# Encoder layer: layer norm of the convolution branch moved to the mixing stage, attention's steps issued further apart, last projections keys instead of values

## The chip, the cores and the metric

One core of a Trainium2 chip. The metric is the device time of one execution in microseconds; the time before is the median of 3 runs. Engines: PE (matmuls, weight loads), DVE (vector), ACT (scalar), POOL (GpSimd), SP (issues most transfers).

## The reference

One layer on 2048 tokens of width 1024, everything in float32. Attention looks at a window of 8 by 16 neighbours on a grid of 32 by 64 tokens, with 8 heads of 64 channels. Beside it runs a convolution branch of 512 channels: `conformer_conv` gates a with sigmoid(g), convolves over 31 positions, takes a layer norm over the 512 channels, and silu. 16 experts follow.

```python
        h = rms_norm(x, norm1_g[l])
        proj = jnp.einsum('bsd,de->bse', h, w_in[l])
        q, k, v, a, g = jnp.split(proj, splits, axis=-1)
        ...
        attn = neighbourhood_attention(q, k, v, rpb[l])
        conv = conformer_conv(a, g, conv_w[l], conv_b[l], conv_ln_g[l], conv_ln_b[l])
        mixed = jnp.concatenate([rms_norm(attn, attn_out_g[l]), rms_norm(conv, conv_out_g[l])], axis=-1)
        x = x + jnp.einsum('bse,ed->bsd', mixed, w_out[l])
        h = rms_norm(x, norm2_g[l])
        x = x + expert_choice_ffn(h, w_router[l], w_gate[l], w_up[l], w_down[l])
    return rms_norm(x, final_g)
```

## The kernel before

Products are made of three matmuls of split operands (`mm3`, L116: a rounded high part and the rest that `split` at L122 leaves). The program is written out in four stages, and each engine takes its instructions in the order of the source.

**Projections.** `jobs` (L376) lists what is projected: queries (`q_part`), keys (`k_part`), values (`v_part`) and the gated input of the convolution (`gate_a`). Results of q, k and v go to DRAM, from SP's queue (q, k) or ACT's (v). Beside them DVE does the 31 taps of the convolution (`conv_block`); `pump` doles them out by estimated time. A finished block of 128 channels is transposed and stored in `dw_scr` (`to_tokens`, put off by `LAG`). The last job is the second half of the values, and its last four parts stand in the attention loop.

**Attention.** 128 tiles: 8 heads, 4 column blocks, 4 row groups. The loop is a pipeline over tiles. Step i issues `transposes` of tile i + LT, `scores` of tile j = i + LS, `normed` of tile j - 1, `rests` of tile i + LT, `values` of tile i. In `scores` PE makes the products, DVE adds the bias and takes the minimum (L530), ACT takes the exponential and its sum (L534). `normed` takes a reciprocal on DVE (L544) and scales the tile (L546), even tiles on DVE, odd ones on POOL. `transposes` is PE, then a copy on ACT (L568). `rests` subtracts that copy on DVE (L573). `values` is PE (L586), and every fourth tile adds the two halves of the output: a copy on ACT (L596) and an addition on DVE (L599), at once.

```python
    LS, LT = 6, 2
```

Per head SP loads queries, keys (two parts), two bias tables and two sets of values, at fixed places in the loop: `load_qk` of the next head at tile 3 of this one, `load_kl` at 5, `load_tb` at 8, `load_v` at 13; `load_tb(h, 1)` at 0 and `load_v(h, 1)` at 3 are this head's own. `load` (L108) makes a transfer wait for the last matmul issued before it. The queries and keys lie in tiles of which one transfer fills 64 partitions, the values' transfers fill 24 or 32, the tables' 128. Tiles of 8 KB per partition come from a pool of 22 (`slot`), small ones from a pool of 8 (`e2`).

**What is done beside attention** is set by the table `on(i, ...)`. In the first 52 tiles it is the layer norm of the convolution branch: load a quarter of `dw_scr` (`conv_load`), statistics (`conv_stats`, L475), normalise (`conv_norm`: L483 on DVE, the gain and offset at L486 and L487 on POOL), store to `y_scr`. From tile 98 on it is loading, scaling (`wo_lead`, L501, POOL) and splitting (`wo_rest`, L506, DVE) of the output projection's weights.

**Mixing** goes over 16 groups of 128 tokens: `stage_y` loads y, `stage_z` takes silu and the sum of squares, `stage_b` transposes, `stage_a` splits the attention output (two groups at a time), `stage_c` multiplies with the weights in two halves, `stage_h`, `stage_d`, `stage_r`, `stage_s` make the router's scores (L710 is a power on POOL), `stage_k`, `stage_l` rank them. **Experts** are the rest, some 2290 us of matmuls.

Of the kernel before, what the change touches and what calls it, by code (L numbers as in the profile page):

```python
# [28 lines left out]
NORM_POOL = 2  # L29
# [25 lines left out]
def kernel(  # L55
# [100 lines left out]
    y_scr = dram.tile([4, P, 4, 512], F32, name="y_scr")  # L156
# [102 lines left out]
    def conv_block(i, u):  # L259

        a = slot([P, T])
        tap_w = lambda k: pv_sb[:, PV_CW + i * 31 + k : PV_CW + i * 31 + k + 1]

        def first():
            nc.vector.tensor_scalar(
                a, u, tap_w(15), pv_sb[:, PV_CB + i : PV_CB + i + 1], op0=ALU.mult, op1=ALU.add
            )

        def tap(k):
            sh = k - 15  # L270
# [5 lines left out]
        def to_tokens(b):  # L276
            ps = bank([P, 4, P])
            for j in range(4):
                tr(ps[:, j, :], a[:, (b * 4 + j) * P : (b * 4 + j + 1) * P], ident)
# [95 lines left out]

    jobs = [("q", 1), ("a", 1), ("q", 2), ("q", 3), ("a", 2), ("k", 0), ("k", 1), ("a", 3), ("k", 2), ("k", 3), ("v", 0), ("v", 1)]  # L376
    ws, raws = {}, {}

    def fetch(n):
# [48 lines left out]
    for n, (kind, i) in enumerate(jobs):  # L428
# [3 lines left out]
        if kind == "a":  # L432
            u = slot([P, T])
        for c in range(4):
# [5 lines left out]
            elif kind == "v":  # L440
                if i == 1 and c == 3:

                    break
# [22 lines left out]
    ys, ymv, wo = {}, {}, {}  # L466

    def conv_load(c):
        ys[c] = slot([P, 4, 512])
        ymv[c] = col(8, tag="mv")  # L470
        load(ys[c], dw_scr[c])

    def conv_stats(c, t):
        bst = col(6, tag="bs")
        nc.vector.bn_stats(bst, ys[c][:, t])  # L475
        nc.vector.bn_aggr(ymv[c][:, 2 * t : 2 * t + 2], bst)

    def conv_rstd(c):
        ymv[c, "r"] = rsqrt_mean(ymv[c].rearrange("p (r k) -> p r k", k=2)[:, :, 1], 1.0, 4)

    def conv_norm(c, t):
        y = ys[c][:, t]
        nc.vector.tensor_scalar(  # L483
            y, y, ymv[c][:, 2 * t : 2 * t + 1], ymv[c, "r"][:, t : t + 1], op0=ALU.subtract, op1=ALU.mult
        )
        nc.gpsimd.tensor_tensor(out=y, in0=y, in1=ln_gb[:, 0], op=ALU.mult)  # L486
        nc.gpsimd.tensor_tensor(out=y, in0=y, in1=ln_gb[:, 1], op=ALU.add)  # L487

    def conv_store(c):
        nc.gpsimd.dma_start(y_scr[c], ys[c])  # L490
# [48 lines left out]
    def normed(i):  # L539
# [5 lines left out]
        eng = nc.gpsimd if i % NORM_POOL else nc.vector  # L545
# [29 lines left out]
    def values(i):  # L575
# [747 lines left out]
```

## Time and profile before

| | |
|---|---|
| median of 3 runs | 3306.64 us (3303.76 to 3307.41) |
| the profiled execution | 3305.04 us |
| its span | 3303.3 us |
| PE busy in the span | 3154.7 us (96%) |
| DVE, ACT, POOL busy | 64%, 41%, 13% |
| attention (465.4 to 777.5 us) | 312.1 us, PE busy 224.3 |
| mixing (777.5 to 1010) | 232.5 us, PE busy 226.7 |

The span runs from the first to the last instruction of the profiled execution; all times of the trace count from its start. Durations below are of this execution, so a sum is made against 3305.04. The averages hide the stages: PE is full in projections, mixing and experts, and not in attention.

### The profile page before, as it was taken

What the parts mean: (1) busy time and instruction counts of PE and PEld (TensorE: products, weight loads), DVE (VectorE), ACT (ScalarE), POOL (GpSimd) and SP (SyncE); (2) the same over time, 40 slices, a digit from 0 to 9 for tenths busy, and PEclk for the clock granted to TensorE, in tenths of its full rate; (3) what the DMA queues carried; (4) which work ended last, traced back from release to release, by engine and by line L of the source; (5) the groups of instructions that cost most, each with busy time, mean ns of one, the idle gap of its engine ahead of it and who ended that gap; (6) DMA issues with size and microseconds to landing.
All of it is one profiled execution on the core that took longest, in us unless ns stands there. A gap on an engine that the chain in (4) does not pass through costs nothing.

```text
span 3303.3 us, 51326 instructions
## 1 busy us (share of the span) xinstructions
PE 3154.7 (96%) x21282; PEld 2890.9 (88%) x21282; DVE 2103.1 (64%) x3235; ACT 1369.5 (41%) x2216; POOL 433.7 (13%) x300
## 2 busy tenths in 40 slices
PE   7999996778997999999999999999999999999998
PEld 6888885667886999999999999999999999999997
DVE  5799967886555687555555555555555555555565
ACT  5111124564332444444444444444444444444454
POOL 2111015544322000000000000000000000000011
PEclk9999997898997999999999999999999999999999
DMA  6222377893344565656656565656656656566585
GB/s 249 61 86 90 112 207 206 226 238 109 119 140 138 200 194 183 212 181 216 195 201 189 194 215 189 199 189 204 204 189 196 203 193 212 177 209 198 198 277 201
DMA packets 394761, 610.88 MB, mean 185 GB/s; under 512 B 14240, under 2 KB 315552, under 8 KB 390304
## 3 DMA queue, kind: packets, MB, share of 16 engines
q1 hardware_dynamic: 358816, 555.11, 51.6%
q0 software_dynamic: 10080, 38.80, 4.5%
q10 hardware_dynamic: 25632, 13.70, 1.4%
q8 instruction: 167, 2.74, 0.4%
q14 instruction: 66, 0.54, 0.1%
HBM read 532.05 MB, written 75.50 MB: 184 GB/s over the span
## 4 chain that ended last, share of the span: by engine, by line
PE 67%; DMA 1%; DVE 0%; ACT 0%; issue 0%; POOLq 0%; POOL 0%; ACTq 0%
PE b L103 66%; PE b L106 1%; DMA s<-acc 0%; DMA s<-h_scr,c 0%; DMA out_dram<-s,c 0%; ACT s L123 0%; DVE s L124 0%; DVE s L1215 0%; DVE e L864 0%; DVE s L1220 0%; POOLq L1319 0%; DVE rd L870 0%; POOL c L144 0%; DVE e L1032 0%; ACT e L123 0%
## 5 line engine op out<-in xcount | busy, mean ns | idle before, releaser
L103 PE MATMUL b<-s,s 128*128 128x256 f32 (+1 forms) x15616 | 2249.3, 302 | 5.4 <-ACT s L211 4.2
L103 PEld LDWEIGHTS b<-s,s 128*128 128x128 f32 x15616 | 2076.1, 192 | 116.3 <-ACT s L211 4.6
L124 DVE TENSOR_TENSOR s<-s,s 128x1024 fp32r<-128x1024 f32 x768 | 896.4, 1221 | 116.0 <-ACT s L123 104.2
L123 ACT ACTIVATE s<-s 128x1024 fp32r<-128x1024 f32 x768 | 755.0, 1046 | 33.8 <-issue 30.1
L103 PE MATMUL b<-s,e 128*128 128x512 f32 x3072 | 746.8, 392 | 0.0
L103 PEld LDWEIGHTS b<-s,e 128*128 128x128 f32 x3072 | 560.6, 189 | 105.7
L1031 ACT ACTIVATE e<-b 128x256 f32<-128x256 f32 x256 | 98.3, 384 | 988.5 <-PE b L103 988.5
L1032 DVE TENSOR_TENSOR e<-e,b 128x256 f32<-128x256 f32 x256 | 107.8, 421 | 578.9 <-ACT e L1031 578.9
L272 DVE SCALAR_TENSOR_TENSOR s<-s,pv_sb,s 128x2033 f32<-128x2033 f32 (+14 forms) x120 | 311.4, 2595 | 2.2
L1061 POOL DMA_INDIRECT acc<-s,c x30 | 53.9, 1796 | 1249.4 <-ACT s L1058 1141.1
L586 PE MATMUL b<-s,s 128*128 128x256 f32 (+3 forms) x512 | 117.1, 331 | 83.0 <-DVE s L573 66.5
L124 DVE TENSOR_TENSOR e<-e,e 128x256 fp32r<-128x256 f32 x256 | 108.8, 425 | 123.8 <-ACT e L123 123.3
L586 PEld LDWEIGHTS b<-s,s 128*128 128x128 f32 (+1 forms) x512 | 93.6, 223 | 107.3 <-DVE s L573 86.0
L123 ACT ACTIVATE e<-e 128x256 fp32r<-128x256 f32 x256 | 106.9, 417 | 130.7 <-DVE e L1032 130.7
L972 POOL DMA_INDIRECT s<-h_scr,c x32 | 56.1, 1753 | 766.3 <-issue 655.6
L534 ACT ACTIVATE e<-e,c 128x384 f32<-128x384 f32 (+2 forms) x128 | 79.4, 620 | 97.7 <-DVE c L544 69.6
L546 POOL TENSOR_SCALAR e<-e,c 128x384 f32<-128x384 f32 (+1 forms) x64 | 82.7, 1292 | 190.4 <-DVE c L544 182.5
L106 PE MATMUL b<-ident,e 128*128 128x128 f32 (+1 forms) x512 | 95.5, 312 | 4.8 <-POOL e L546 4.1
L124 DVE TENSOR_TENSOR s<-b,s 128x512 fp32r<-128x512 f32 x80 | 52.4, 687 | 70.3 <-ACT s L123 70.3
L530 DVE CUSTOM_DVE_ANT_0 e<-b,s 128x384 f32<-128x384 f32 (+2 forms) x128 | 71.1, 556 | 24.5 <-PE b L103 24.0
L123 ACT ACTIVATE e<-b 128x256 fp32r<-128x256 f32 (+1 forms) x48 | 21.8, 454 | 145.8 <-PE b L103 96.2
L573 DVE TENSOR_TENSOR s<-b,s 128x384 fp32r<-128x384 f32 (+3 forms) x128 | 77.6, 606 | 6.5 <-ACT s L568 6.5
(140 smaller groups left out, 1520.3 us busy)
## 6 DMA issues: line engine op xcount, KB each, us to landing
s<-in_w_gate_dram SPq DMA_DIRECT2D x128, 1024.0 KB
s<-in_w_up_dram SPq DMA_DIRECT2D x128, 1024.0 KB
s<-in_w_down_dram SPq DMA_DIRECT2D x128, 1024.0 KB
s<-in_x_dram SPq DMA_DIRECT2D x8, 1024.0 KB
s<-in_xT_dram SPq DMA_DIRECT2D x8, 1024.0 KB
v_scr<-e ACTq DMA_DIRECT2D x32, 256.0 KB
s<-kh_scr SPq DMA_DIRECT2D x16, 512.0 KB
s<-kl_scr SPq DMA_DIRECT2D x16, 512.0 KB
```

The lines of the kernel that those rows point to most:

```text
L103: pe[0] = nc.tensor.matmul(o, l, r, start=start, stop=stop)
L106: pe[0] = nc.tensor.transpose(o, i, idt)
L123: nc.scalar.activation(hi, src, AF.Copy)
L124: nc.vector.tensor_tensor(lo, src, hi.bitcast(F32), op=ALU.subtract)
L272: nc.vector.scalar_tensor_tensor(a[:, s:e], u[:, s + sh : e + sh], tap_w(k), a[:, s:e], op0=ALU.mult, op1=ALU.add)
L530: nc.vector.tensor_tensor_reduce(out=s[:, :n], in0=ps[:, :n], in1=bt[:, boff : boff + n], scale=-1.0, scalar=3.0e38, op0=ALU.add, op1=ALU. ...
L534: nc.scalar.activation(s[:, :n], s[:, :n], AF.Exp, bias=nm[:, rg : rg + 1], scale=-1.0, accum_out=rs_[:, rg : rg + 1])
L546: eng.tensor_scalar(s[:, :n], s[:, :n], ri, None, op0=ALU.mult)
L573: nc.vector.tensor_tensor(lo, src, hi.bitcast(F32), op=ALU.subtract)
L586: nc_mm = nc.tensor.matmul(o[:, r0 : r0 + nr], vt[:nk, g], part[:nk, at : at + nr], start=g == 0 and p == 0, stop=g == 7 and p == 1, skip_ ...
L1031: nc.scalar.activation(s, ps[:, 0], AF.Silu)
L1032: nc.vector.tensor_tensor(s, s, ps[:, 1], op=ALU.mult)
```

## The change

- The layer norm leaves attention's table. `dw_scr` itself is loaded in the mixing stage (`stage_y`, a quarter at a time), each group of 128 tokens is normalised there (`stage_n`, `stage_o`), three groups ahead of `stage_c`; the first three stand in attention's tiles 117 to 121. `y_scr` is gone.
- The order of jobs: values are done before the last two key blocks, which are one job ("kk") done side by side; their last quarter stands in the attention loop at steps -5 and -3. Head 0's loads are issued from the start of that job on.
- `LS, LT` become 7, 3, and the halves of the output are copied one tile later (`out_copy`) and added two tiles later (`out_add`).
- Tiles below 100 are all scaled on POOL; from 100 on even ones on DVE as before.
- `stage_a` splits one group at a time; the convolution's accumulator is taken from the pool when it is first used; the last block's `to_tokens` come after 5 instead of 9.

```diff
-NORM_POOL = 2
+NORM_POOL = 100
...
-                later.append((now[0] + LAG + 4 * b, lambda b=b: to_tokens(b)))
+                later.append((now[0] + (LAG if i < 3 else 5) + 4 * b, lambda b=b: to_tokens(b)))
...
-    jobs = [("q", 1), ("a", 1), ("q", 2), ("q", 3), ("a", 2), ("k", 0), ("k", 1), ("a", 3), ("k", 2), ("k", 3), ("v", 0), ("v", 1)]
+    jobs = [("q", 1), ("a", 1), ("q", 2), ("q", 3), ("a", 2), ("k", 0), ("a", 3), ("k", 1), ("v", 0), ("v", 1), ("kk", 2)]
...
+        if kind == "kk":
+            load_qk(0)
...
+            elif kind == "kk":
+                if c == 3:
+
+                    break
+                for s in range(2):
+                    k_part(i + s, w[s], c)
+                    pump(4.4)
+                if c == 0:
+                    load_kl(0)
+                    load_tb(0, 0)
+                    load_v(0, 0)
+                    load_tb(0, 1)
...
-        eng = nc.gpsimd if i % NORM_POOL else nc.vector
+        eng = nc.gpsimd if i < NORM_POOL or i % 2 else nc.vector
...
         if k == 3:
             del pts[h, cb]
...
+            on(i + 1, lambda: out_copy(h, cb))
+            on(i + 2, lambda: out_add(h, cb))
...
-    def stage_y(t):
-        ym[t] = e2([P, 512])
-        nc.sync.dma_start(ym[t], y_scr[t // 4, :, t % 4])
+    def stage_y(c):
+        ym[c] = slot([P, 4, 512])
+        nc.sync.dma_start(ym[c], dw_scr[c])
+
+    def stage_n(t):
+
+        st = col(8, tag="mv")
+        nc.vector.bn_stats(st[:, 0:6], ym[t // 4][:, t % 4])
+        nc.vector.bn_aggr(st[:, 6:8], st[:, 0:6])
+        yn[t] = (st[:, 6:7], rsqrt_mean(st[:, 7:8], 1.0))
+
+    def stage_o(t):
+
+        y = ym[t // 4][:, t % 4]
+        mu, r = yn.pop(t)
+        nc.vector.tensor_scalar(y, y, mu, r, op0=ALU.subtract, op1=ALU.mult)
+        nc.gpsimd.tensor_tensor(out=y, in0=y, in1=ln_gb[:, 0], op=ALU.mult)
+        nc.gpsimd.tensor_tensor(out=y, in0=y, in1=ln_gb[:, 1], op=ALU.add)
...
-    LS, LT = 6, 2
...
-    for c in range(4):
-        o = 12 * c
-        on(o, lambda c=c: conv_load(c))
-        for t in range(4):
-            on(o + 7 + t, lambda c=c, t=t: conv_stats(c, t))
-            on(o + 12 + t, lambda c=c, t=t: conv_norm(c, t))
-        on(o + 10, lambda c=c: conv_rstd(c))
-        on(o + 16, lambda c=c: conv_store(c))
+    LS, LT = 7, 3
...
+    for t in range(3):
+        on(117 + t, lambda t=t: stage_n(t))
+        on(119 + t, lambda t=t: stage_o(t))
...
-        if -4 <= i < 0:
-            v_part(1, *w, 16 + i)
+        if i in (-5, -3):
+            k_part(2 + (i == -3), w[i == -3], 3)
...
     for t in range(0, 16):
-        if t + 3 < 16:
-            stage_y(t + 3)
         if t + 1 < 16:
             stage_b(t + 1)
-        if t % 2 == 1 and t < 15:
-            stage_a((t + 1) // 2)
+        if t + 3 < 16:
+            stage_n(t + 3)
         if t >= 1:
             stage_h(t - 1)
-        if t + 2 < 16:
-            stage_z(t + 2)
+        if t + 1 < 16:
+            stage_a(t + 1)
         if t >= 2:
             stage_s(t - 2)
         stage_c(t, 0)
+        if t + 3 < 16:
+            stage_o(t + 3)
+        if t % 4 == 0 and t < 12:
+            stage_y(t // 4 + 1)
+        if t + 2 < 16:
+            stage_z(t + 2)
```

SP's queue where projections end, before (`raw` is a weight tile, `s` a tile of the pool of 22, the sources are DRAM):

```order
L222 DMA raw_2386<-in_w_in_dram 128x8x256
L110 DMA s_2992<-qh_scr 64x2048
L110 DMA s_2992<-ql_scr 64x2048
L110 DMA s_2995<-kh_scr 64x2048 x2
L110 DMA s_2998<-kl_scr 64x2048 x2
L110 DMA s_3125<-in_tb_dram 128x1920
L110 DMA s_3127<-in_tb_dram 128x1280
L110 DMA s_3129<-v_scr 24x1024 x8
L110 DMA s_3373<-v_scr 32x1024 x8
L110 DMA s_3382<-qh_scr 64x2048
```

and of the change:

```order
L221 DMA raw_2603<-in_w_in_dram 128x8x256
L110 DMA s_3092<-qh_scr 64x2048
L110 DMA s_3092<-ql_scr 64x2048
L110 DMA s_3095<-kh_scr 64x2048 x2
L320 DMA kh_scr<-e_3123 128x512
L321 DMA kl_scr<-e_3124 128x512
L320 DMA kh_scr<-e_3155 128x512
L321 DMA kl_scr<-e_3156 128x512
L110 DMA s_3161<-kl_scr 64x2048 x2
L110 DMA s_3164<-in_tb_dram 128x1920
L110 DMA s_3166<-v_scr 24x1024 x8
L110 DMA s_3175<-in_tb_dram 128x1280
```

Head 0's values are read after a whole job of keys instead of right after the last values are written; stores of keys for heads 4 to 7 now stand between the loads.

DVE in two tiles of attention with a head's output due, before (line 483 is the layer norm):

```order
L530 ISA e_4402,c_4370<-b_4399,s_4160 128x512
L530 ISA c_4370 128x1
L544 RECIPROCAL c_4405<-c_4371 128x1
L546 TENSOR_SCALAR e_4375<-e_4375,c_4405 128x384
L573 TENSOR_TENSOR s_4366<-b_4393,s_4365 96x2x2x128
L599 TENSOR_TENSOR s_3279<-b_4329,e_4411 64x32x16
L530 ISA e_4423,c_4370<-b_4420,s_4160 128x512
L530 ISA c_4370 128x1
L544 RECIPROCAL c_4426<-c_4371 128x1
L573 TENSOR_TENSOR s_4366<-b_4414,s_4365 96x2x2x128
L483 TENSOR_SCALAR s_4128<-s_4128,c_4129,c_4391 128x512
```

and of the change (517, 531, 560, 597 are the former 530, 544, 573, 599):

```order
L517 ISA e_4478,c_4473<-b_4475,s_4288 128x288
L517 ISA c_4473 128x1
L531 RECIPROCAL c_4481<-c_4377 128x1
L560 TENSOR_TENSOR s_4469<-b_4464,s_4468 128x3x128
L597 TENSOR_TENSOR s_3334<-b_4360,e_4462 64x32x16
L517 ISA e_4499,c_4473<-b_4496,s_4288 128x384
L517 ISA c_4473 128x1
L531 RECIPROCAL c_4502<-c_4474 128x1
L560 TENSOR_TENSOR s_4469<-b_4490,s_4468 128x2x2x128
```

The scaling and the layer norm are gone from DVE here, and the addition of the output's halves stands two tiles after the values it adds.

POOL in one step of mixing, before:

```order
L710 TENSOR_TENSOR c_6832<-euler,c_6832 128x16
L144 TENSOR_TENSOR rcnorm<-c_6851,nhalf 128x1
L144 TENSOR_TENSOR ranorm<-c_6882,nhalf 128x1
L144 TENSOR_TENSOR c_6956<-c_6954,nhalf 128x1
L710 TENSOR_TENSOR c_6969<-euler,c_6969 128x16
```

and of the change (725 is the former 710; 630 and 631 are the gain and offset):

```order
L725 TENSOR_TENSOR c_6910<-euler,c_6910 128x16
L144 TENSOR_TENSOR c_6927<-c_6925,nhalf 128x1
L144 TENSOR_TENSOR ranorm<-c_6968,nhalf 128x1
L630 TENSOR_TENSOR s_6574<-s_6574,gains 128x512
L631 TENSOR_TENSOR s_6574<-s_6574,gains 128x512
L144 TENSOR_TENSOR rcnorm<-c_6993,nhalf 128x1
L144 TENSOR_TENSOR c_7052<-c_7050,nhalf 128x1
L725 TENSOR_TENSOR c_7065<-euler,c_7065 128x16
```

Two passes over 512 elements and one more small power stand in POOL's queue in every step, ahead of the power for the convolution half's norm two groups on (`rcnorm`) and of the one for the router's norm (`c`).

## Rows read from the trace of the kernel before

**Rows 1.** The page's part 1: busy time, share of the span, instructions.
```profile
PE 3154.7 (96%) x21282; PEld 2890.9 (88%) x21282; DVE 2103.1 (64%) x3235; ACT 1369.5 (41%) x2216; POOL 433.7 (13%) x300
```

**Rows 2.** Windows: attention, then mixing. Columns: stretch, length, busy (count) by engine, PEclk, DMA share, GB/s.
```profile
465.40:777.50 312.10, 224.31 (x1315) 198.36 (x1312) 244.04 (x683) 177.53 (x431) 157.80 (x122) 0.84 0.79 220
777.50:1010.00 232.50, 226.68 (x1305) 193.11 (x1305) 126.90 (x303) 76.49 (x206) 61.62 (x57) 0.98 0.35 121
```

**Rows 3.** Windows between the starts of heads' loads; then two heads together, and the end.
```profile
485.55:531.95 46.40, 28.00 (x150) 25.37 (x151) 28.96 (x84) 20.94 (x52) 13.94 (x11) 0.71 0.69 192
531.95:571.03 39.08, 28.24 (x139) 24.98 (x139) 34.84 (x91) 20.64 (x51) 27.63 (x23) 0.73 0.83 231
571.03:610.86 39.83, 28.66 (x152) 25.02 (x151) 32.44 (x90) 20.73 (x51) 24.48 (x21) 0.79 0.81 246
610.86:648.46 37.60, 27.43 (x160) 24.27 (x160) 32.16 (x90) 22.19 (x57) 22.60 (x19) 0.86 0.80 206
648.46:706.96 58.50, 44.97 (x307) 38.73 (x305) 50.23 (x152) 42.18 (x106) 20.23 (x17) 1.00 0.91 227
706.96:777.50 70.54, 51.02 (x291) 44.85 (x289) 58.21 (x153) 42.96 (x102) 46.67 (x33) 0.84 0.68 199
```

**Rows 4.** Timeline of SP's queue: head 0's values, then the loads that cut rows 3.
```profile
469.90 15.60 SPq L110 DMA_DIRECT2D s<-v_scr  x16
485.55 0.46 SPq L110 DMA_DIRECT2D s<-qh_scr  x1
531.95 0.45 SPq L110 DMA_DIRECT2D s<-qh_scr  x1
```

**Rows 5.** Timeline, attention's start, ACT and PE: start, us, instruction, idle before it.
```profile
505.74 0.59 ACT L596 ACTIVATE e<-b 64x512 f32<-64x512 f32 x1 [10.07 <-DMA v_scr<-e]
487.99 1.73 PE L586 MATMUL b<-s,s 96*128 96x256 f32 x4 [3.60 <-ACT s L568]
507.00 0.58 PE L586 MATMUL b<-s,s 96*128 96x256 f32 x1 [9.69 <-ACT s L568]
```

**Rows 6.** Groups of the attention stage (465.4 to 777.5): the scalings of line 546.
```profile
L546 POOL TENSOR_SCALAR e<-e,c 128x384 f32<-128x384 f32 (+1 forms) x64 | 82.7, 1292 | 190.4 <-DVE c L544 182.5 <-DMA v_scr<-e 3.3 <-DMA s<-ql_scr 2.9
L546 DVE TENSOR_SCALAR e<-e,c 128x288 f32<-128x288 f32 (+1 forms) x64 | 38.4, 600 | 2.3
```

**Rows 7.** Waits in the same two heads.
```profile
PE b L586 <- DVE s L573: 13.4, 22, 1.0
```

**Rows 8.** Groups of the attention stage: the convolution branch's layer norm.
```profile
L475 DVE BATCH_NORM_STATS2 c<-s 128x6 f32<-128x512 f32 x16 | 10.9, 683 | 0.1
L483 DVE TENSOR_SCALAR s<-s,c,c 128x512 f32<-128x512 f32 x16 | 14.7, 917 | 0.0
L486 POOL TENSOR_TENSOR s<-s,gains 128x512 f32<-128x512 f32 x16 | 20.5, 1284 | 1.5 <-DVE s L483 1.5
L487 POOL TENSOR_TENSOR s<-s,gains 128x512 f32<-128x512 f32 x16 | 21.1, 1317 | 1.3
```

**Rows 9.** Timeline of DVE around 530 us: one operation beside a free and a busy POOL.
```profile
544.06 0.42 DVE L546 TENSOR_SCALAR e<-e,c 128x384 f32<-128x384 f32 x1
528.00 1.37 DVE L546 TENSOR_SCALAR e<-e,c 128x384 f32<-128x384 f32 x1
```

**Rows 10.** Windows of 6 us: DMA while 64-partition and 128-partition tiles are loaded.
```profile
548.00:554.00 6.00, 4.42 (x29) 3.76 (x29) 5.83 (x18) 3.37 (x9) 3.10 (x3) 1.00 0.97 388
686.00:692.00 6.00, 4.02 (x27) 3.28 (x26) 5.57 (x16) 4.14 (x11) 1.56 (x1) 1.00 1.01 218
```

**Rows 11.** Mixing stage by form (POOL, DVE), and 24 matmuls of a PE timeline.
```profile
L710 POOL TENSOR_TENSOR c<-euler,c 128x16 f32<-128x16 f32 x13 | 37.8, 2909 | 0.0
L682 DVE SCALAR_TENSOR_TENSOR s<-s,c,gains 128x1024 f32<-128x1024 f32 x14 | 17.9, 1277 | 0.0
804.17 5.71 PE L103 MATMUL b<-s,s 128*128 128x512 f32 x24
```

More of the change, by code (lines that the diff above doesn't have):

```diff
@@ L440 @@
             elif kind == "v":
-                if i == 1 and c == 3:
-                    break
                 for t in range(4):
@@ L463 @@
     attn = [slot([P, T]) for _ in range(4)]
[L466 to L490, printed above, removed]
+    wo = {}
     def wo_load(b):
@@ L506, in wo_rest, with on @@
         nc.vector.scalar_tensor_tensor(lo, raw, g, hi.bitcast(F32), op0=ALU.mult, op1=ALU.subtract)
+    beside = {}
+    def on(i, *fs):
+        beside.setdefault(i, []).extend(fs)
     tiles = [(h, cb, rg) for h in range(H) for cb in CBO for rg in range(4)]
-    st_p, st_ps, pts, sums, outs = {}, {}, {}, {}, {}
+    st_p, st_ps, pts, sums, outs, rest_out = {}, {}, {}, {}, {}, {}
     def scores(i):
@@ L626, in stage_z, with stage_b @@
         yr[t] = rsqrt_mean(ss[:, 0:1], 512, r=rcnorm[:, t : t + 1])
-    def stage_a(u):
-        ts_ = slice(u * 256, (u + 1) * 256)
-        m = slot([P, 2, 4, 256], F32R)
-        for b in range(4):
-            nc.scalar.activation(m[:, 0, b], attn[b][:, ts_], AF.Copy)
-            nc.vector.tensor_tensor(m[:, 1, b], attn[b][:, ts_], m[:, 0, b].bitcast(F32), op=ALU.subtract)
-        for t in range(2):
-            ma[2 * u + t] = m[:, :, :, t * P : (t + 1) * P]
+    def stage_b(t):
+        y = ym[t // 4][:, t % 4]
+        if t % 4 == 3:
+            ym.pop(t // 4)
+        m = slot([P, 2, 2, 4, P], F32R)
+        ma[t], mc[t] = m[:, 0], m[:, 1]
+        ps = bank([P, 4, P])
+        for j in range(4):
+            tr(ps[:, j, :], y[:, j * P : (j + 1) * P], ident)
+        split(m[:, 1, 0], m[:, 1, 1], ps)
@@ L638, in stage_q, with stage_a, token_norm @@
+    def stage_a(t):
+        ts_ = slice(t * P, (t + 1) * P)
+        for b in range(4):
+            nc.scalar.activation(ma[t][:, 0, b], attn[b][:, ts_], AF.Copy)
+            nc.vector.tensor_tensor(ma[t][:, 1, b], attn[b][:, ts_], ma[t][:, 0, b].bitcast(F32), op=ALU.subtract)
+    def token_norm(sq, r):
+        ps = bank([P, 2])
+        for b in range(4):
+            mm(ps[:, 0:1], sq[:, b], one, b == 0, b == 3)
+        return rsqrt_mean(ps[:, 0:1], 512, r=r)
     def stage_q(t):
@@ L642, in stage_q @@
             nc.scalar.activation(sq[:, b], attn[b][:, t * P : (t + 1) * P], AF.Square)
-        ps = bank([P, 2])
-        for b in range(4):
-            mm(ps[:, 0:1], sq[:, b], one, b == 0, b == 3)
-        ara[t] = rsqrt_mean(ps[:, 0:1], 512, r=ranorm[:, t : t + 1])
-    def stage_b(t):
-        y = ym.pop(t)
-        if t % 2 == 0:
-            m = slot([P, 2, 2, 4, P], F32R)
-            mc[t], mc[t + 1] = m[:, 0], m[:, 1]
-        m = mc[t]
-        ps = bank([P, 4, P])
-        for j in range(4):
-            tr(ps[:, j, :], y[:, j * P : (j + 1) * P], ident)
-        split(m[:, 0], m[:, 1], ps)
+        ara[t] = token_norm(sq, ranorm[:, t : t + 1])
     def stage_c(t, n, first=0):
@@ L813 @@
         for f in beside.pop(i, []):
+            f()
+    for i in sorted(beside):
+        for f in beside.pop(i):
             f()
```

65 lines of the change are left out of this document (32 added, 33 removed).

## The prediction

> **What bounds the kernel now.** I read the page's busy times first, then windows by stage and by head, then waits, timelines and groups. PE is busy 96% of the span [rows 1], but not evenly: in attention 224.3 of 312.1 us, in mixing 226.7 of 232.5 [rows 2]. So some 88 us can be had in attention, and hardly any in mixing. Each window by head begins where SP issues the next head's loads (its tile 3) and holds 16 tiles, but for the last [rows 3]. The first has start-up in it: 46.4 us. The next three, under which the layer norm runs, take 39.1, 39.8 and 37.6 us; the two after it together 58.5, or 29.25 each, 1.83 us a tile; the last holds 34 tiles and the scaling of the output weights, 70.5 us [rows 3]. [...]
>
> What limits those two quiet heads? In 58.5 us, 32 tiles: DVE is busy 50.2, PE 45.0, ACT 42.2, POOL 20.2, and the DMA share is 0.91 [rows 3]. No engine is full. PE waits 22 times for the subtraction of line 573, 13.4 us in all [rows 7]: values of tile i need the subtraction of tile i + 1, which DVE finished only one step before.
>
> **Start.** SP's queue stands 15.6 us on head 0's values [rows 4], because these are the last thing projected and written. Then ACT waits 10.1 us for a small buffer that a transfer of values still holds, the copy of the output halves stands in front of the copy that PE wants, and PE waits 9.7 us there and 3.6 us before [rows 5].
>
> **The change, part by part.**
>
> *Start and head 0 (465.4 to 531.95, 66.6 us [rows 2, 4]).* With keys last, head 0's values are written a whole job before they are used (six key parts, by 5.7 us some 34), and the output's copy no longer stands in line with the tile's own. The two key parts in the loop are 24 matmuls of 512 columns each, 5.7 us [rows 11], the same PE work as the four value parts. Then: 11.4 for those, 2.5 for the scores beside them, 15 tiles at 1.7 (below) 25.5, and 4 for transfers that are still behind (key stores, two convolution stores, head 0's and head 1's loads follow each other): 43.5. **Minus 23.** Bounds: 38 if nothing is behind, 54 if half of the loss stays.
>
> *Layer norm out of heads 1 to 3, scalings on POOL, LT = 3.* First what each resource needs per tile afterwards, from the quiet heads. DVE: 50.2 less 16 scalings of 0.600 [rows 6] is 40.6, over 32 tiles 1.27. POOL: 20.2 and 16 more of 1.292 [rows 6] is 40.9, 1.28. ACT 1.32, PE 1.41 at full clock [rows 3]. Transfers: 0.91 of 58.5 us is 53.2, 26.6 a head, 1.66 a tile, and the bytes of a head don't change. So the transfers become the longest. The step between tiles i + 1 and i is one longer, so PE's 13.4 us of waits [rows 7] should go, and DVE no longer waits for a copy that was issued just ahead of its addition. I take 27.0 a head, 1.69 a tile: the transfers and a little over. This floor is real: with a share near 1 the rate is 218 GB/s while queries and keys come in, 388 where whole 128-partition tiles do [rows 10].
>
> [...]
>
> Heads 1 to 3 (531.95 to 648.46): 116.5 becomes 81. **Minus 35.5.** Heads 4 and 5: 58.5 becomes 54. **Minus 4.5.** Bounds for a head: 29.25 as now without layer norm (87.8 and 58.5), and PE's own 22.6 (67.7 and 45.1).
>
> *The last 34 tiles and the end of attention, 70.5 us.* DVE is busy 58.2, POOL 46.7 [rows 3]. Three groups of layer norm come in: on DVE 3 x (0.68 + 0.92, and by estimate 0.4 of small ones) = 6, on POOL 3 x (1.28 + 1.32, and by estimate 0.6 for the power) = 9.6 [rows 8]. DVE goes to 64, POOL to some 57 with the last scalings below tile 100. The longer lead takes out some waits, the fuller POOL delays some weights. **0**, from minus 6 to plus 8.
>
> *Mixing, 232.5 us.* Thirteen steps of 14.5 us gain 2 us of DVE and 3.2 of POOL. DVE was busy 126.9/16 = 7.9 a step, POOL 3.9 [rows 2]: 9.9 and 7.1 of 14.5. The work runs three groups ahead of the matmuls that need it, so PE covers it; if that cover were gone it would cost the rival below. Splitting `stage_a` per group only halves the instructions' width. **Plus 1**, from 0 to plus 8. The 8 MB that no longer pass in attention (four loads and four stores of 1 MB) come back in mixing as 4 MB of loads, where the DMA share is 0.35 [rows 2].
>
> *Nothing:* projections (same matmuls, PE full), experts, the convolution's taps (same count before the last block ends).
>
> **Sum:** -23 - 35.5 - 4.5 + 0 + 1 = -62, so 3305 - 62 = **3243 us**. The profiled execution (3305.04) lies 1.6 below the median of the runs; I make no correction for that.
>
> **The rivals.**
>
> *A, the transfers are no floor.* If loads that were issued late now overlap better and PE sets the pace at some 1.5 us a tile (1.41 and a tenth for semaphores), a head takes 24: heads 1 to 5 save 55 instead of 40, the start 25, together 3305 - 80 + 1 = 3226. For it: no wait on loads shows in the quiet heads. Against: their share of 0.91. [...]
>
> *B, the waits only change places.* Tiles go no faster than in the quiet heads, 1.83 us, since ACT, DVE and PE still hand each tile round and POOL's 1.29 us replaces 0.600 in the chain. Then heads 1 to 3 save 28.8, 4 and 5 nothing, the start 18, the end costs 3: 3305 - 47 + 4 = 3262. For it: no engine was full at 1.83.
>
> *C, slower.* POOL in mixing. A step's layer norm is 2 us on DVE and 3.2 on POOL, one after the other, and beside POOL's passes over 512 elements a DVE operation can be held up: a scaling of 384 elements took 0.42 us beside an idle POOL and 1.37 beside a busy one [rows 9]. DVE's 1.28 us product of line 682 [rows 11], on which the transposes for the router hang, could wait for a pass of 1.3. If all of that comes onto PE's path, 13 x (5.2 + 1.3) = 84: 3243 + 84 = 3327. It decides from the point where POOL's queue, with its 2.9 us power of line 710 [rows 11], is late by more than the slack of a step; at 7 of 14.5 us it isn't.
>
> [...]
>
> **How the numbers follow.** The forecast has 0.61, A 0.15, B 0.20, C 0.04. With every bound at its bad end the sum is 3280, with every one at its good end 3208. The range takes in A and B; it keeps the bad end, since the start and the pace of the tiles could both disappoint, and stops short of the good one, which needs all at once: **3222 to 3280**. A difference of 0.2%, 6.6 us, is about what a measurement can tell from none. All cases but C are faster: faster 0.94, same 0.02, slower 0.04.
>
> **What would show it.** Right: attention some 250 us long instead of 312; SP no longer standing on head 0's values; PE's waits for line 573 (now 560) nearly gone; 16 tiles in 27 us with a DMA share of 0.97 or more, and in place of the old waits PE waiting for keys, queries or tables at a head's first tiles; a granted clock near 1.00 in all heads; POOL busy near 0.75 of attention; mixing within 8 us of 232. Wrong: heads at 29 us with a share below 0.9 (B), at 24 (A), or PE gaps in mixing behind POOL (C). If the start still costs over 50 us, I misread what held it.

## The result, and the profile after

| | before | changed |
|---|---|---|
| median of 4 runs | 3305.20 us (3299.07 to 3307.41) | 3261.09 us (3256.80 to 3264.74) |
| ratio, 95% interval | | 0.9869 [0.9850, 0.9888] |
| the profiled execution | 3305.04 us | 3264.74 us |
| its span | 3303.3 us | 3263.0 us |

The change makes the kernel 1.3% faster, 44 us by the medians and 40.3 by the two profiled executions. The forecast was 62 us, to 3243. The profiled execution of the changed kernel is the slowest of its four, so a time read from it lies a little on the high side.

The page's busy times of the changed kernel (columns as in [rows 1]):

```profile
PE 3137.8 (96%) x21282; PEld 2880.2 (88%) x21282; DVE 2082.9 (64%) x3229; ACT 1368.9 (42%) x2248; POOL 500.8 (15%) x358
```

PE has 17 us less of busy time for the same 21282 matmuls; the granted clock over the span is 0.981 against 0.977 before. The windows of the changed kernel, cut as in [rows 3] where SP issues the next head's loads:

```profile
489.62:522.55 32.93, 23.41 (x154) 21.44 (x152) 19.12 (x67) 18.85 (x49) 19.03 (x15) 0.84 0.91 223
522.55:551.03 28.48, 22.72 (x131) 20.07 (x130) 19.09 (x63) 19.23 (x49) 19.14 (x16) 0.84 0.93 231
551.03:579.59 28.56, 23.07 (x152) 21.09 (x151) 20.93 (x68) 20.83 (x54) 20.02 (x16) 0.92 0.95 234
579.59:609.00 29.41, 24.22 (x167) 22.29 (x166) 22.04 (x70) 21.71 (x56) 21.09 (x17) 0.94 0.97 225
609.00:638.99 29.99, 23.85 (x151) 21.20 (x150) 19.79 (x67) 19.53 (x50) 19.37 (x16) 0.89 0.90 219
638.99:668.97 29.98, 24.70 (x152) 21.70 (x150) 20.86 (x68) 20.39 (x53) 19.83 (x17) 0.89 0.89 223
```

Heads 1 to 3 become 8 to 11 us shorter each (39.1, 39.8 and 37.6 before); heads 4 and 5 do not become shorter in this execution (29.25 before). DVE falls from 35 of 39 us to 19 of 28, so it is no longer the fullest. No engine is full now; what comes nearest to full is the DMA share, 0.89 to 0.97.

DVE's waits of the changed kernel from 440 to 760 us (what was waited for, us in total, times, longest):

```profile
DVE e L517 <- DMA s<-in_tb_dram: 34.7, 7, 7.3
DVE e L517 <- DMA kh_scr<-e: 6.8, 1, 6.8
DVE e L517 <- DMA kl_scr<-e: 5.1, 4, 3.0
```

and PE's in the same stretch:

```profile
PE b L106 <- POOL e L533: 29.9, 33, 5.6
PE b L573 <- DVE s L560: 18.2, 19, 6.7
PE b L103 <- DMA s<-kl_scr: 17.5, 7, 4.5
```

Seven times DVE waits for a bias table and seven times PE for the low parts of the keys: about once a head, at its first tiles. The wait for `rests` is down to 18.2 us from 66.5 over the whole of attention (of which [rows 7] are the two quiet heads). The scaling on POOL (L533) is a new wait of PE; 19.5 us of it remain in the run below in which no head after the first loads anything.

The parts between marks that both traces have; "mixing" begins here at the first matmul of a token norm and ends at the first expert's silu:

| part | forecast | before | after | difference |
|---|---|---|---|---|
| start and head 0 (465.4 to head 1's first cut) | -23 | 66.55 | 57.15 | -9.4 |
| heads 1 to 3 | -35.5 | 116.51 | 86.45 | -30.1 |
| heads 4 and 5 | -4.5 | 58.50 | 59.97 | +1.5 |
| last head, up to mixing | 0 | 76.60 | 83.71 | +7.1 |
| mixing | +1 | 287.74 | 279.12 | -8.6 |
| experts | 0 | 2232.0 | 2231.2 | -0.8 |

Each column is one execution. How far a part can differ between two executions shows in the run "silu early" below, whose attention is the same program: its first four parts take 55.79, 86.14, 56.64 and 84.34 us. Heads 4 and 5, of which the window is

```profile
607.33:663.97 56.64, 46.77 (x299) 41.68 (x297) 41.16 (x135) 40.30 (x102) 39.28 (x32) 0.91 0.94 234
```

are 1.9 us shorter than before there, where the table has them 1.5 us longer: their difference is not clear of this scatter.

### The profile page after: what moved, and what is told of

Same layout as the page of the kernel before. It is cut to its first block, busy times and chain, and to the rows that moved or that the text cites. A ratio compares the mean times of both kernels' runs of the same rounds, so it can differ in the third digit from the quotient of the medians.

```text
span 3263.0 us, 51574 instructions
## 1 busy us (share of the span) xinstructions
PE 3137.8 (96%) x21282; PEld 2880.2 (88%) x21282; DVE 2082.9 (64%) x3229; ACT 1368.9 (42%) x2248; POOL 500.8 (15%) x358
## 4 chain that ended last, share of the span: by engine, by line
PE 86%; DMA 5%; DVE 5%; issue 2%; POOL 1%; SPq 1%; ACT 0%; POOLq 0%; ACTq 0%; DVEq 0%
PE b L103 83%; DVE s L272 3%; PE b L106 2%; DMA s<-kl_scr 2%; DMA s<-in_tb_dram 1%; DMA s<-v_scr 1%; SPq L110 1%; POOL e L533 0%; POOL s L483 0%; PE b L573 0%; DMA s<-kh_scr 0%; DMA s<-in_xT_dram 0%; DMA gains<-in_rows_dram 0%; DVE s L488 0%; DVE e L124 0%
## 5 line engine op out<-in xcount | busy, mean ns | idle before, releaser
L533 POOL TENSOR_SCALAR e<-e,c 128x384 f32<-128x384 f32 (+2 forms) x114 | 143.8, 1269 | 130.5 <-DVE c L531 58.1
L573 PE MATMUL b<-s,s 128*128 128x256 f32 (+3 forms) x512 | 96.3, 310 | 18.4 <-DVE s L560 18.2
L106 PE MATMUL b<-ident,e 128*96 128x128 f32 (+1 forms) x448 | 81.6, 304 | 30.1 <-POOL e L533 29.9
L517 DVE CUSTOM_DVE_ANT_0 e<-b,s 128x384 f32<-128x384 f32 (+2 forms) x128 | 71.1, 555 | 52.1 <-DMA s<-in_tb_dram 34.7
L106 PEld LDWEIGHTS b<-ident,e 128*96 128x96 f32 (+1 forms) x448 | 52.6, 144 | 41.0 <-POOL e L533 38.5
```

What stands on the lines that cost most here:

```text
L106: pe[0] = nc.tensor.transpose(o, i, idt)
L517: nc.vector.tensor_tensor_reduce(out=s[:, :n], in0=ps[:, :n], in1=bt[:, boff : boff + n], scale=-1.0, scalar=3.0e38, op0=ALU.add, op1=ALU. ...
L533: eng.tensor_scalar(s[:, :n], s[:, :n], ri, None, op0=ALU.mult)
L573: nc_mm = nc.tensor.matmul(o[:, r0 : r0 + nr], vt[:nk, g], part[:nk, at : at + nr], start=g == 0 and p == 0, stop=g == 7 and p == 1, skip_ ...
```

## The experiments

Two theories were set against each other. **L**: loads set a head's pace. Its transfers take 26 to 28 us and are issued at fixed tiles, so PE and DVE wait at a head's first tiles. **E**: the engines set it, handing each tile round. Times are medians; ratios are to the kernel before, taken on the same chip. The two that alter the result (one table, no loads) are clocks for a part, not kernels to use.

| run | us | ratio, 95% interval | heads 1 to 5, mean us |
|---|---|---|---|
| the change | 3261.09 | 0.9869 [0.9850, 0.9888] | 29.3 |
| one table for all heads | 3245.42 | 0.9812 [0.9796, 0.9829] | 26.0 |
| loads issued earlier | 3259.45 | 0.9862 [0.9845, 0.9878] | 27.6 |
| even scalings on DVE | 3258.64 | 0.9856 [0.9839, 0.9872] | 28.3 |
| lead 6, 2 | 3258.84 | 0.9855 [0.9839, 0.9872] | 29.6 |
| layer norm back | 3288.68 | 0.9946 [0.9929, 0.9963] | 36.2 |
| values last | 3262.06 | 0.9869 [0.9848, 0.9890] | 27.9 |
| no loads after head 0 | 3224.73 | 0.9756 [0.9736, 0.9777] | 24.6 |
| start's queue | 3251.25 | 0.9838 [0.9817, 0.9859] | 28.1 |
| silu early | 3268.06 | 0.9892 [0.9864, 0.9919] | 28.6 |
| key copies | 3245.32 | 0.9822 [0.9795, 0.9849] | 27.2 |
| key copies, early loads | 3243.55 | 0.9817 [0.9791, 0.9844] | 27.1 |
| half the copies | 3241.53 | 0.9808 [0.9793, 0.9823] | 26.0 |

### What sets a head's pace

**One table for all heads.** In the loop:

```diff
-                    load_tb(h + 1, 0)
+                    tbs[h + 1, 0] = tbs[0, 0]
...
-                load_tb(h, 1)
+                tbs[h, 1] = tbs[0, 1]
```

> The changed kernel, but all heads use head 0's two bias tables, so 1.6 MB a head is not loaded (the bias of heads 1 to 7 is therefore another). Theory L, loads set the pace of a head: the changed kernel's heads take 28.5 to 30 us and DVE waits 34.7 us in all for tables at seven heads' starts; without them a head has 5 of 6.6 MB to load, some 23 us by its own rate, so 16 tiles in 23.5 to 25.5 us and the kernel 22 to 35 us faster. Theory E, the hand-over between engines sets it (1.83 us a tile as in the quiet heads before): 16 tiles stay at 28 to 30 us, the kernel within 6 us of the changed one.

**Loads issued earlier.** From head 1 on, values' second set at tile 1 instead of 3, queries and keys at 2 instead of 3, the keys' low parts at 3 instead of 5; the first table at 6 instead of 8 everywhere:

```diff
-            if k == 3:
+            if k == (1 if h else 3):
                 load_v(h, 1)
...
-                if k == 8:
+                if k == 6:
                     load_tb(h + 1, 0)
```

> The changed kernel with a head's loads issued earlier: values' second set at tile 1 instead of 3, queries and keys of the next head at 2 instead of 3, the keys' rest at 3 instead of 5, the first table at 6 instead of 8. Theory L with gaps in the transfers because loads are tied to tiles that themselves wait: the DMA share over the heads rises from 0.93 to 0.96 or more, a head takes 27 to 28 us, the kernel is 6 to 15 us faster. Theory L without gaps (the share is already all there is): within 4 us. Theory E: within 4 us, and the share doesn't rise.

**No loads after head 0.**

```diff
...
             if h and k == 0:
-                load_tb(h, 1)
+                heads[h] = heads[0]
+                tbs[h, 0], tbs[h, 1] = tbs[0, 0], tbs[0, 1]
+                for b in range(4):
+                    vts[h, b] = vts[0, b]
```

> Heads 1 to 7 work on head 0's queries, keys, values and bias tables, so that no head after the first loads anything (that part is left out; the output differs). What remains is the pace of the engines alone. Theory L: heads 1 to 5 take 22.6 to 24.5 us (PE's own time at full clock and a tenth of semaphores), attention shortens by 25 to 40 us: 3220 to 3236. Theory E: they take 27 us or more, 3245 to 3255.

Heads 1 to 5 in one window, the change, then the runs with one table, early loads and, in a stretch that holds 65 tiles, no loads:

```profile
522.55:668.97 146.42, 118.57 (x745) 106.35 (x744) 102.71 (x335) 101.70 (x257) 99.45 (x80) 0.90 0.93 226
```
```profile
517.31:647.21 129.90, 112.13 (x759) 100.52 (x759) 104.25 (x339) 102.86 (x259) 99.70 (x80) 0.96 0.85 193
```
```profile
518.30:656.38 138.08, 114.49 (x759) 102.25 (x758) 104.72 (x343) 103.79 (x262) 101.12 (x81) 0.95 0.96 241
```
```profile
520.00:620.00 100.00, 91.28 (x612) 78.08 (x612) 84.07 (x274) 82.44 (x211) 80.57 (x65) 1.00 0.00 1
```

The last has its pace from the starts of L517's operations (durations in ns, first and last start):

```profile
L517 DVE CUSTOM_DVE_ANT_0 e<-b,s x64: 444/544/693, 530.4 to 627.3; 128x384 f32<-128x384 f32 x32, 128x288 f32<-128x288 f32 x16, 128x512 f32<-128x512 f32 x16
```

63 steps in 96.9 us are 1.54 us a tile, 24.6 a head: the engines' own pace, with PE busy 91% at full clock. The changed kernel's 29.3 is 4.7 above it, and without loads the kernel is 36 us faster. That is L, within the time it gave (3220 to 3236); the head is at the upper edge of L's 22.6 to 24.5. With one table a head takes 26.0 us and the time is 16 us better than the changed kernel's: less than L had said on both counts (23.5 to 25.5, and 22 to 35 us), but E had no place for any of it. What keeps these heads from 24.6 was not taken apart; 10.3 us of PE's waits for keys remain over the five. Early loads bring the profiled heads to 27.6, but that execution (3253.32) is the fastest of its four, and the medians differ by 1.6 us: inconclusive.

### What the parts of the change were worth

**Even scalings on DVE**, as before the change:

```diff
-NORM_POOL = 100
+NORM_POOL = 2
```

> The changed kernel with even tiles' scalings on DVE again in all of attention. Theory L: DVE then has some 1.5 us a tile, still under the 1.8 of the loads, so heads stay at 28.5 to 30 us and the kernel within 5 us. Theory E, with POOL's longer scaling in the chain of a tile: heads become shorter by 1 us or more and the kernel 5 to 10 us faster. If DVE's work was what the change took away: 10 us or more slower.

**Lead 6, 2**, as before the change:

```diff
-    LS, LT = 7, 3
+    LS, LT = 6, 2
```

> The changed kernel with the leads of before, LS 6 and LT 2. Theory L: PE's waits for the subtraction come back inside a head, but take the place of the waits for loads at its start; 0 to 8 us slower. Theory E: the longer lead is what shortened the tiles; 15 to 30 us slower, heads at 31 us or more.

Both parts are worth nothing here: 0.9856 and 0.9855 against 0.9869, intervals overlapping. DVE's fill in heads 1 to 5 goes from 0.70 to 0.87 with the scalings back, and heads do not get longer:

```profile
518.88:660.50 141.62, 115.74 (x754) 104.75 (x753) 123.29 (x378) 102.03 (x261) 50.53 (x40) 0.93 0.94 235
```

With the old lead the wait for `rests` comes back and costs nothing. PE's waits in that run, 440 to 760 us:

```profile
PE b L573 <- DVE s L560: 31.1, 45, 5.7
PE b L103 <- DMA s<-kl_scr: 14.5, 7, 4.1
PE b L106 <- POOL e L533: 6.5, 3, 4.0
```

The three add up to 52.1 us, against 65.6 in the changed kernel, and the time is the same. Which wait PE stands in has changed, and not the time. Whether either part is worth something in a kernel whose heads do not wait for loads was not tried.

**Layer norm back** under heads 0 to 3, from `y_scr` into mixing, everything else as changed:

```diff
-        nc.sync.dma_start(ym[c], dw_scr[c])
+        nc.sync.dma_start(ym[c], y_scr[c])
...
-    for t in range(3):
-        on(117 + t, lambda t=t: stage_n(t))
-        on(119 + t, lambda t=t: stage_o(t))
+    for c in range(4):
+        o = 12 * c
+        on(o, lambda c=c: conv_load(c))
+        for t in range(4):
+            on(o + 7 + t, lambda c=c, t=t: conv_stats(c, t))
+            on(o + 12 + t, lambda c=c, t=t: conv_norm(c, t))
+        on(o + 10, lambda c=c: conv_rstd(c))
+        on(o + 16, lambda c=c: conv_store(c))
...
-        if t + 3 < 16:
-            stage_n(t + 3)
...
-        if t + 3 < 16:
-            stage_o(t + 3)
```

> The layer norm goes back under heads 0 to 3 of attention and out of the mixing stage; values before keys, the longer steps, the scalings on POOL and the order of the mixing stage stay as in the change. Theory L (loads set a head's pace, and the layer norm had been DVE's and POOL's load on top): heads 1 to 3 go back from 28.7 us to 36 to 40 each, with POOL now the fullest (scalings 20.6 us and layer norm some 15 a head), mixing gains nothing, in all 22 to 32 us slower than the changed kernel: 3283 to 3293. Theory E (the hand-over between engines, which the longer steps and the POOL scalings loosened, gave the gain): heads stay within 31, under 8 us slower: 3261 to 3269.

Heads 1 to 3 of that run:

```profile
522.43:563.63 41.20, 27.15 (x147) 23.40 (x148) 30.31 (x85) 21.71 (x53) 38.07 (x31) 0.78 0.83 237
563.63:608.40 44.77, 32.82 (x164) 29.71 (x164) 29.59 (x89) 22.24 (x54) 39.63 (x34) 0.67 0.75 218
608.40:646.00 37.60, 28.60 (x171) 26.01 (x170) 26.46 (x79) 22.09 (x55) 33.69 (x27) 0.77 0.79 207
```

25 us (0.0077 of the ratio) come from the layer norm's place, with all scalings on POOL. It is POOL that fills here, 0.89 to 0.92 of each head, where DVE did before [rows 3]; beside the old scalings the layer norm may cost another sum, which was not tried. Mixing takes 279.5 us in this run without the layer norm, 279.1 with it: in mixing it costs nothing that shows.

The 25 us are a difference of two parts. Heads 1 to 3 take 123.7 us in this run against 86.5 in the changed kernel, 37 us more. But the last head, up to mixing, is 10 us shorter without the three groups of layer norm that the change puts into tiles 117 to 121. This run, then the changed kernel:

```profile
703.46:777.01 73.55, 53.00 (x306) 46.27 (x305) 64.71 (x170) 47.39 (x118) 46.58 (x33) 0.87 0.70 207
```
```profile
668.97:752.68 83.71, 56.54 (x310) 48.98 (x309) 73.56 (x185) 48.43 (x121) 56.78 (x43) 0.78 0.61 182
```

So the thirteen groups in mixing cost nothing that shows, and the three at attention's end some 10 us. Where else these three could stand was not tried.

**Values last**, the old order of jobs, with head 0's loads at their old places in it:

```diff
-... ("k", 0), ("a", 3), ("k", 1), ("v", 0), ("v", 1), ("kk", 2)]
+... ("k", 0), ("k", 1), ("a", 3), ("k", 2), ("k", 3), ("v", 0), ("v", 1)]
...
-        if i in (-5, -3):
-            k_part(2 + (i == -3), w[i == -3], 3)
+        if -4 <= i < 0:
+            v_part(1, *w, 16 + i)
```

> The order of the last projections goes back (keys, then values last, four value parts inside the loop); all else as in the change. If the order made the start shorter, SP stands on head 0's values for 15 us again and the stretch from the last projections to head 1 is 8 to 12 us longer: 3269 to 3273. If it was only the layer norm leaving head 0 that shortened it, the time stays within 3 us of 3261.

The order is worth nothing here, though SP's row of head 0's values, its 16 issues included, is longer than before the change (22.86 us against 15.60 [rows 4]). SP's queue in this run:

```profile
464.98 22.86 SPq L110 DMA_DIRECT2D s<-v_scr  x16
487.88 0.46 SPq L110 DMA_DIRECT2D s<-qh_scr  x1
523.52 0.45 SPq L110 DMA_DIRECT2D s<-qh_scr  x1
```

The cut at 523.52 lies within 1 us of the changed kernel's 522.55. The 10 us wait for a buffer of values is back too:

```profile
509.91 0.59 ACT L580 ACTIVATE e<-b 64x512 f32<-64x512 f32 x1 [11.06 <-DMA v_scr<-e]
```

So one stall was exchanged for another, and the changed kernel's comes from key stores. Its SP queue, DVE and PE (start, us, instruction, idle before it):

```profile
492.09 0.55 SPq L320 DMA_DIRECT2D kh_scr<-e  x1
```

```profile
505.60 0.69 DVE L517 CUSTOM_DVE_ANT_0 e<-b,s 128x512 f32<-128x512 f32 x1 [6.80 <-DMA kh_scr<-e]
```
```profile
507.01 1.01 PE L573 MATMUL b<-s,s 128*128 128x256 f32 x3 [6.67 <-DVE s L560]
510.99 0.58 PE L103 MATMUL b<-s,s 128*128 128x288 f32 x1 [2.01 <-DMA s<-kl_scr]
```

DVE wants one of the eight small buffers, and by the profile a store of keys still holds it; SP issued the last of these stores at 492.1 us, behind the loads of head 1's queries and keys (from 489.62). Whether the order of jobs is worth something once this stall is gone was not tried.

**Start's queue.** The last four key parts are stored by ACT, and 1 MB of gains, which nothing needs before tile 117, is loaded at tile 100, with the router's weights:

```diff
-                    k_part(i + s, w[s], c)
+                    k_part(i + s, w[s], c, nc.scalar if c == 2 else None)
...
-    nc.scalar.dma_start(gains, rows[0:2048].partition_broadcast(P))
...
-    nc.scalar.dma_start(wr, w_router.rearrange("p (d e) -> p d e", d=8))
...
+    on(100, lambda: nc.sync.dma_start(gains, rows[0:2048].partition_broadcast(P)))
+    on(100, lambda: nc.sync.dma_start(wr, w_router.rearrange("p (d e) -> p d e", d=8)))
...
-            k_part(2 + (i == -3), w[i == -3], 3)
+            k_part(2 + (i == -3), w[i == -3], 3, nc.scalar)
```

> The stores of the last four key parts are issued by ACT and not by SP, and the 1 MB of gains and the router's weights are loaded at tile 100 and not at the end of the projections. If key stores that stand behind loads hold DVE's buffers (6.8 and 5.1 us in head 0) and the start is short of transfer time, the stretch to head 1 falls from 57 us to 44 to 50: 3248 to 3254. If the transfers all have to pass anyway before head 1 can begin, it gains under 4 us: 3257 to 3262.

The stretch to the cut falls from 57.2 to 47.9 us (to 513.26), as expected, and the time is 10 us below the changed kernel's. The two intervals overlap a little; of the single runs none does (3250.09 to 3251.74 against 3256.80 to 3264.74). So these two things were a part of what held the start. Which of them did how much was not tried apart, but the trace has a place for both. Of the 9.3 us, 6.0 are gained before SP issues head 1's loads (at 483.65 instead of 489.62): there, in the changed kernel, SP stands 10.7 us before a store of keys, and by the profile what ends this is the landing of the gains. The other 3.3 are gained in head 0, where DVE's 6.8 us wait for a store of `kh_scr` is gone. SP's longest wait in the changed kernel from 465 to 523 us:

```profile
SPq L320 <- DMA gains<-in_rows_dram: 10.7, 1, 10.7
```

**Silu early**, the old place of `stage_z` in a step of mixing:

```diff
+        if t + 2 < 16:
+            stage_z(t + 2)
         if t >= 2:
             stage_s(t - 2)
         stage_c(t, 0)
...
-        if t + 2 < 16:
-            stage_z(t + 2)
```

> Only the place of the silu and the squares of the tokens after next goes back ahead of the step's first matmuls; the layer norm stays in the mixing stage. If that order (and not the layer norm) is what made mixing shorter, PE waits for ACT's squares of line 672 again, some 6 us in all, and the time is 4 to 9 us longer than the changed kernel: 3265 to 3270. If the order is worth nothing: 3258 to 3263.

Mixing takes 287.7 us in this run, as before the change, and 278.5 to 282.4 in the twelve profiles with the changed order. The time is 7 us longer, with overlapping intervals. PE waits 4.0 us in 13 places for the squares of `stage_q` on ACT, which stand behind that silu (5.8 in the kernel before, 0.3 in the changed one). So mixing's gain is this order. Of the 8.6 us some 4.3 are idle time of PE and 4.3 its busy time, for the same 1576 matmuls. From the first token norm to the first expert's silu, the changed kernel and this run:

```profile
752.68:1031.80 279.12, 258.96 (x1576) 223.59 (x1575) 185.73 (x462) 87.34 (x243) 118.61 (x102) 0.94 0.36 125
```
```profile
748.31:1036.00 287.69, 263.28 (x1576) 223.66 (x1576) 187.92 (x465) 87.86 (x246) 118.14 (x103) 0.93 0.35 122
```

### A version that beats both

**Key copies.** On top of the start's queue, keys of heads 1 to 7 are loaded into 64 partitions, and copied to the other 64 at tiles 12 to 15:

```diff
+    def key_copy(h, n):
+        cs = slice(n * 512, (n + 1) * 512)
+        kh, kl = heads[h][1:]
+        nc.scalar.activation(kh[64:128, cs], kh[0:64, cs], AF.Copy)
+        nc.vector.tensor_copy(kl[64:128, cs], kl[0:64, cs])
```

> The kernel with the start's stores on ACT, and from head 1 on each key tensor is loaded into 64 partitions only; ACT and DVE copy it to the other 64 in four pieces of 512 columns. A head moves 1 MB less, 4.8 us at 218 GB/s. Theory L (loads set the pace): heads 1 to 5 fall from 28.1 us to 24 to 26, in all 12 to 25 us less: 3226 to 3239. Theory E (engines' hand-over): the copies add 0.57 us of ACT and about as much of DVE to four tiles of each head, and nothing or a loss comes of it: 3249 to 3258.

**Key copies, early loads**: the same with the earlier tiles for loads.

> The same, and each head's loads issued some tiles earlier, as in the run with early loads. If what is left at a head's first tiles is loads that were issued late, 3 to 10 us below the run with the copies alone. If the copies have already made the loads early enough, within 3 us of it.

It is 1.8 us below the run with the copies alone (3243.55 against 3245.32), and a head takes 27.1 us against 27.2: the second case held.

**Half the copies**: as the last, but only the low parts are copied, two pieces by ACT, two by DVE.

```diff
-        nc.scalar.activation(kh[64:128, cs], kh[0:64, cs], AF.Copy)
-        nc.vector.tensor_copy(kl[64:128, cs], kl[0:64, cs])
+        if n % 2:
+            nc.vector.tensor_copy(kl[64:128, cs], kl[0:64, cs])
+        else:
+            nc.scalar.activation(kl[64:128, cs], kl[0:64, cs], AF.Copy)
```

> The version that takes the best of all: start's stores on ACT, early loads, and only the low parts of the keys copied on the chip (two pieces by ACT, two by DVE); the high parts are loaded twice again. If the copies had made ACT and DVE the bound (with them a head took 27 us at a DMA share of 0.8, without any loads 24.6), halving them gives heads of 25.5 to 26.5 and 3 to 8 us less than with all copies: 3235 to 3241. If the loads come back as the bound at a share of 0.88 or more, it is no faster: 3243 to 3251.

Heads 1 to 5 with the start's queue, with all copies, and with half of them and early loads:

```profile
513.26:653.75 140.49, 117.48 (x752) 102.87 (x750) 103.58 (x339) 101.83 (x258) 99.45 (x80) 0.94 0.95 236
```
```profile
512.48:648.55 136.07, 117.46 (x759) 98.65 (x758) 115.03 (x360) 115.55 (x280) 101.77 (x81) 0.99 0.80 206
```
```profile
510.46:640.48 130.02, 112.58 (x748) 95.64 (x748) 109.83 (x346) 107.91 (x265) 98.77 (x79) 1.00 0.94 235
```

With all copies the share falls to 0.80, no wait of DVE or PE for tables and keys is left in these heads, and the clock is 0.99. Yet a head still takes 27.2 us. The copies put 13.7 us on ACT and 11.4 on DVE over five heads, and the time falls between the two expectations: the engines take back most of what the loads give. Half the copies have the lowest median of the kernels that do all of the work, 3241.53 us, 0.9808 of the kernel before and 0.6% below the changed one. A head takes 26.0 us, as the first case said; the time is half a microsecond above that case's range, and the share is back at 0.94, at which the second case had expected no gain. The three versions with copies lie within each other's intervals; that the half is better than the whole rests on the heads of one profile each.

## Why the prediction was right, and where it was wrong

The sign and the range held: 3261 lies inside 3222 to 3280, 18 us above the forecast, and on the figure of rival B (3262). Part of this is luck. Attention gave 31 of the 63 us that were forecast for it, and mixing, of which nothing was expected, gave 8.6. B's price was no better founded: it had 18 us for the start, where 9.4 came, and a loss in mixing. Heads take 29 us as B said, but at a share of 0.93 and with waits for tables and keys at a head's first tiles, which the prediction listed as signs of the forecast's own floor. Without loads the engines do 24.6, where B had them at 29. A's tenth for semaphores was an estimate that no run shows by itself; its whole step, 1.5 us a tile, is 1.54 without loads.

Of the 43 us that the ratio gives, single undoings account for 25 (the layer norm's place) and 7 to 8 (the order in mixing). The rest is of the size of the gain in start and head 0, and which part of the change made that stays open.

Two rows that the list uses: what ended SP's longest stop from 469.9 to 486 us in the kernel before, and DVE's product for the router in the changed one, 742 to 1020 us.

```profile
SPq L110 <- DMA gains<-in_rows_dram: 6.0, 1, 6.0
```
```profile
L697 DVE SCALAR_TENSOR_TENSOR s<-s,c,gains 128x1024 f32<-128x1024 f32 x16 | 20.4, 1278 | 1.0 <-POOL c L144 0.8 <-issue 0.3
```

- **Start and head 0, -23: this step failed most.** It is -9.4, beyond the bound of 54 us for the stretch (57.2). The step rested on SP standing 15.6 us on head 0's values [rows 4] and on ACT's wait for their buffer [rows 5]. It misread the first: those 15.6 us are 16 issues with stops between them, and the longest stop, 6.0 us, ends by the profile with the landing of the gains; the stops that end with a store of values are 2.6 us together, after one of 9.7 us just ahead of the row. The change left the gains where they were, and by the profile SP stands on them again, for 10.7 us. The wait of ACT went, but one for key stores took its place, and putting the values last again costs nothing. The stretch of the changed kernel is also short of transfer time: the share is 0.91 over all of it, 1.02 from 490 to 500 us and 1.05 from 500 to 507. The term had 4 us for "transfers that are still behind"; moving the gains and the last key stores away gave 9.3 more. Of the single undoings (values, lead, scalings, layer norm) none brings head 0's window above 36 us, where it took 46.4 before and 32.9 after the change: how the parts share the gain stays open.
- **Heads 1 to 3, -35.5: right in kind, -30.1.** Layer norm back shows that its place alone is worth 37 us in these heads, beside scalings on POOL. Transfers do hold a head (over heads 1 to 5 it takes 29.3 us with loads, 24.6 without), but 27.0 took them as back to back. They are tied to tiles, so each head leaves gaps, and the share was 0.93, not 0.97 and over. The rate while queries and keys come in is that of [rows 10], 218 GB/s at a share of 1.01: in the changed kernel, from 494 to 500 us, with queries and keys under way and a share of 1.00, 213 GB/s were moved (first window of the last section). What makes it lower than the 388 of [rows 10] no run shows.
- **Heads 4 and 5, -4.5: wrong, +1.5** in this execution and -1.9 in that of silu early, so about nothing. The 13.4 us of [rows 7] were named as what should go. They went, and waits for loads came in their place; the old lead gives the same time with those waits back.
- **Scalings on POOL: the sum was right, the effect nil.** DVE has 102.7 us of work in five heads, where it has 123.3 with the even scalings back, and was not what a head waited for.
- **Last tiles, 0: inside its bounds, but mis-sized, +7.1.** The three groups of layer norm at attention's end cost some 10 us there by the run without them, where the step had set the longer lead against them. PE's longest wait in this part, 5.59 us at 695.84 us on POOL, is not theirs: POOL itself had stood 5.3 us on a load of the output weights, and does so for 6.1 us with the layer norm back too.
- **Mixing, +1: wrong sign, -8.6.** The layer norm costs nothing there (279.1 us with it, 279.5 without), as the cover of three groups was to give. The step overlooked that the change also puts `stage_z` behind the first half of `stage_c`, and PE's waits for ACT's squares go from 5.8 us to 0.3.
- **Rival C** did not happen. POOL was busy 124 of 278 us from 742 to 1020 us, and DVE's product (now L697) takes 1278 ns in the mean, as in [rows 11]. No run shows a price of POOL's passes in mixing, which takes 279.1 us with the layer norm and 279.5 without. The 1.37 us of [rows 9] are the time of one operation beside a busy POOL; that POOL held it was the author's reading, and no run tries it.

## What to carry to other kernels

Before a wait is counted as a gain, ask what is late next, and above all whether the transfers of that stretch already fill it: clocking the stage once without its loads (24.6 us a head against 29.3) would have told both the floor and the prize. Before a row of a queue is called a wait, ask what ended each stop in it. A reordering that is made for one engine moves the queues of all: the best surprise of this change, 7 us, was a silu that no longer stood in front of a square. Work that is moved should go all the way: thirteen groups of the layer norm cost nothing in mixing, and the three that stayed at attention's end cost 10 us. Look at what stands in a queue ahead of a store whose buffer is wanted, and move loads that nothing needs soon out of a full stretch: the two together gave 10 us.

## What was not expected of the hardware

In one stall of the changed kernel the granted clock fell to 0.50. PE stood 6.67 us before 507.01. Windows of the changed kernel before, during and after it (last columns PEclk, DMA share, GB/s):

```profile
494.00:500.00 6.00, 6.00 (x45) 5.54 (x44) 4.00 (x13) 4.55 (x12) 4.93 (x4) 1.00 1.00 213
500.00:507.00 7.00, 0.34 (x4) 0.15 (x2) 1.41 (x5) 0.62 (x1) 0.46 (x1) 0.79 1.05 245
507.00:511.00 4.00, 1.97 (x8) 1.58 (x8) 2.33 (x8) 3.58 (x10) 3.86 (x3) 0.50 0.90 236
511.00:515.00 4.00, 4.00 (x20) 4.00 (x21) 0.56 (x4) 0.00 (x0) 0.00 (x0) 0.58 0.74 190
```

From 494 to 500 us PE was busy throughout at a granted clock of 1.00. From 507 to 511 us the clock was 0.50, and from 511 to 515 it was 0.58 in the mean: 0.50 until 514, then 0.64 and 1.00 in the two half microseconds that follow. In that last window PE was the only engine with much to do, but this does not show that the others waited for the slow PE. DVE's idle time there ends with a bias table:

```profile
514.44 0.46 DVE L517 CUSTOM_DVE_ANT_0 e<-b,s 128x288 f32<-128x288 f32 x1 [5.04 <-DMA s<-in_tb_dram]
```

So what the lower clock cost is not shown here. The heads agree with the same picture: with load stalls their clock is 0.84 to 0.94 in the changed kernel, and without them (no loads, all or half of the copies, or heads 4 and 5 before the change [rows 3]) it is 0.99 to 1.00. That the stalls are the cause was not tried by itself. The forecast had counted on a clock near 1.00 and given it no term.
